# Two layer-norm entries and the row products of a feed-forward, put in another order in a two-layer hybrid network

## The chip, the cores and the metric

The kernel runs on one core of a Trainium2 chip. The metric is device time in microseconds (us) of one execution; the kernel before takes 2463.92 us, the median of three runs.

TensorE (PE) multiplies, VectorE (DVE), ScalarE (ACT) and GpSimd (POOL) do the rest, and SyncE (SP) issues most transfers. Each engine works through its own queue in order.

## The reference

The network has two layers on 256 latent and 256 context tokens of width 1024. The first mixes with multi-head latent attention, the second with a gated delta rule; each ends in a gated feed-forward of width 2816. A second part of the second layer ("block 2") follows. What matters here is how a layer wraps its mixer: both residual additions are post-normalised and gated by rows that come from a conditioning vector, and the result is modulated before the next matmul.

```
y = layer_norm(alpha * x + gate * mixer(h), ln_g, ln_b)     # alpha = (2 * DEPTH) ** 0.25
h = modulate(y, shift, scale)                               # y * (1 + scale) + shift
z = layer_norm(alpha * y + gate2 * swiglu(h), ln2_g, ln2_b)

def layer_norm(x, g, b):
    mu = mean(x); var = mean((x - mu) ** 2)
    return (x - mu) * rsqrt(var + 1e-5) * g + b
```

The six rows of each layer (shift, scale and gate, twice) are products of the conditioning vector with a matrix of 1024 x 1024 for each row.

## The kernel before

Tokens are worked in tiles of 128 rows. Every weight and every activation that goes into a matmul is split into a high and a low part: `split` (L119) casts the high part on ScalarE (L125) and subtracts it on VectorE (L126). A product is then three matmuls: high by high (L159), low by high (L160), high by low (L161).

**A layer-norm entry.** `resid` (L520 and on) multiplies the projection by the gate (`y`, L524), adds it to the residual (L526, or L528), and takes the statistics of 512 columns (L530), twice for a tile. `ln_norm` (L334) aggregates them (`BN_AGGR`, L329), scales the variance (L165, VectorE), takes its power of -1/2 on GpSimd (L166; `self.pow` is that instruction), makes the bias -mean * r on VectorE (L338), and normalises the tile in place on ScalarE (L339). `mod_in` (L310) transposes the tile on PE in two groups of four (L317), modulates each block on its way out of PSUM, in turn on VectorE (L324) and ScalarE (L322), into a scratch tile `half`, and splits it (`xh`, `xl`). The plain layer-norm rows are applied to the residual later, by `ln_affine` (L341): four slices, a multiply and an addition each on GpSimd (L345, L346), in place, after the transposes have read the tile.

**Where it happens.** In layer 0 there are four token tiles `res_2401` to `res_2404`, in pairs; `ln` inside `layer0` does a pair. `fin1`, `late` and `fin2` call it: the entry to layer 0's feed-forward (stages `fin1`, `late`), and the entry of the delta-rule layer (`fin2`). In layer 1 two streams, one for each tile (`t` of 0 and 1: `x_11602`, `x_11603`), run `st_all`; its `post1` is the entry of the feed-forward, and `mid` the affine step after it.

**Row products.** The conditioning rows of the next layer are made beside layer 0's feed-forward. `mod_tick` (L271) loads a matrix of 128 x 1024 (`mraw`, SyncE's queue, three buffers) and multiplies it by the broadcast conditioning row on VectorE with an accumulator (`mjunk`, L281). These products get a lower priority (`later(200)`) and are put in the queue behind the instruction in `self.hold`. The feed-forward works in units of hidden columns: weight splits (`lo`), hidden product `hf` (L183) and its split (`hl`). At the start of each unit `step` asks for 5 or 8 products.

**What sets the order.** A scheduler orders each engine's instructions by priority and by its own estimate of when the operands are there; `high_priority` raises a block, and `issue_after(i)` sets a block behind instruction i in that order. The scheduler works on the whole program, so an edge at one place can move instructions of other places.

Of the kernel before, what the change touches and what calls it, by code (L numbers as in the profile page):

```python
# [30 lines left out]
class Net:  # L31
# [88 lines left out]
    def split(self, src, hi, lo, hi_eng=None):  # L120
        nc = self.nc
        if hi_eng == "v":
            nc.vector.tensor_copy(hi, src)
        else:
            nc.scalar.copy(hi, src)  # L125
        self.tail = nc.vector.tensor_tensor(lo, src, hi.bitcast(F32), ALU.subtract).ins  # L126

    def wload(self, src, A, B, parts=2, local=False, raw=None):
# [205 lines left out]
    def ln_norm(self, x, st):  # L334
        nc = self.nc
        m, r = self.ln_stats(st)
        nb = self.tiny(1, "p_nbias")
        nc.vector.scalar_tensor_tensor(nb, m, -1.0, r, ALU.mult, ALU.mult)  # L338
        nc.scalar.activation(x, x, AF.Identity, bias=nb, scale=r)  # L339

    def ln_affine(self, x, g, b):  # L341
# [268 lines left out]
    def layer0(self, stk):  # L610
        nc, a = self.nc, self.a
        sid = [1, 1, 0, 0]
        xT = self.first_in()
        self.crow = [self.mp.tile([P, D], F32, name=f"crow{i}") for i in range(2)]
        for r, src in zip(self.crow, (a["c"][0], a["c_ctx"])):
            nc.scalar.dma_start(r, src.unsqueeze(0).to_broadcast([P, D]))
            nc.scalar.activation(r, r, AF.Silu)
        j2 = self.mod_start(0, 2)
        j3 = self.mod_start(0, 3)
        j45 = []  # L620

        def mid():
            j45.extend(self.mod_start(0, c) for c in (4, 5))

        def step(i):
            self.hold = self.tail
            self.mod_tick(1)

        oT = self.mla(xT, mid, step)
        m2, m3, m4, m5 = j2, j3, *j45  # L630
        pool = stk.enter_context(self.tc.tile_pool(name="res1", bufs=1, reuse_waits="tile"))
        res = [pool.tile([P, D], F32, name=f"res{s}") for s in range(4)]
        for s in range(4):
            nc.sync.dma_start(res[s], a["x" if s > 1 else "ctx"][(s % 2) * P:(s % 2) * P + P])
        with self.phase("l0b"):
            def ln(pair, acc, lnrow, ab, first):
                for i in range(2):
                    s = 2 * pair + i
                    st = self.bn_st()
                    self.resid(res[s], acc[i], gates[s], first, st)  # L640
                    self.ln_norm(res[s], st)
                    self.mod_in(res[s], oT, s * P, ab, sid[s])
                if lnrow:
                    with self.tc.issue_after(self.pow):
                        for s in (2 * pair, 2 * pair + 1):
                            self.ln_affine(res[s], *lnrow)

            ln1 = self.row(a["ln1_g"][0]), self.row(a["ln1_b"][0])
            while self.mq and self.mq[0][1] < 5:
                self.mod_tick(1)  # L650
            ab = self.mod_ab(m3, m4, (0, 0))
            gr = [self.gate_row(m2, s) for s in range(2)]
            gates = [gr[i] for i in sid]
            held = []

            def fin1(pair, acc):
                if pair == 0:
                    ln(pair, acc, ln1, ab, True)
                else:
                    held.append(acc)  # L660

            def late():
                ln(1, held[0], ln1, ab, True)
                self.hold = self.tail
                jn.extend(self.mod_start(1, c) for c in range(2))
                gr = [self.gate_row(m5, s) for s in range(2)]
                gates[:] = [gr[i] for i in sid]

                ln2.extend([self.row(a["ln2_g"][0]), self.row(a["ln2_b"][0])])

            def fin2(pair, acc):
                ln(pair, acc, ln2 if pair else None, ab2, False)

            def step(u):
                if u == NU // 2:
                    jl.extend(self.mod_start(1, c, (0,)) for c in range(2, 6))
                self.mod_tick(5 if u < NU // 2 else 8)
                if u == NU // 2:
                    ab2.extend(self.mod_ab(*jn, (0, 1)))

            jn, jl, ln2, ab2 = [], [], [], []
            self.out_pairs(oT, a["mla_out"], KD, fin1)
            self.ffn512(oT, a["w_ffg"], a["w_ffu"], a["w_ffd0"], res, gates, late, step, fin2)
            self.mods1 = jl
        self.hl = self.dp.tile([NT * P, D], F32, name="hl_spill")
        for t in range(NT):
            nc.gpsimd.dma_start(self.hl[t * P:(t + 1) * P], res[2 + t])
        return oT
# [495 lines left out]
    def st_all(self, t):  # L1184
# [7 lines left out]
        def post1(acc):  # L1192
            with self.tc.high_priority():
                st = self.bn_st()
                self.resid(x, acc, gate(m2), True, st)
                self.ln_norm(x, st)
                self.mod_in(x, self.xT, t * P, ab(), 0)

        def mid():
            self.ln_affine(x, *rows("ln1"))  # L1200
# [668 lines left out]
```

## Time and profile before

| | |
|---|---|
| runs, us | 2463.92, 2468.24, 2463.59 |
| profiled execution, us | 2464.18 |
| its span, us | 2462.4 |
| mean granted TensorE clock | 0.977 |
| busy share: PE, DVE, ACT, POOL | 94%, 70%, 51%, 9% |
| row products (L281) | 128, 156.0 us in all |

The attention layer runs to about 250 us, layer 0's projection and feed-forward to about 673, the delta-rule layer to about 1196, and the rest is layer 1's feed-forward and block 2. The span is the time from the first to the last instruction; the device time has a little around it. A long busy share of PE says how little there is to gain on the whole, and the idle time in a timeline says where it stands.

### The profile page before, as it was taken

How to read it: one execution, taken by the hardware profiler on the slowest of the kernel's cores; microseconds unless marked ns; L12 is line 12 of the kernel's file. 1: busy time of each engine (PE TensorE's matmuls, PEld its weight loads, DVE VectorE, ACT ScalarE, POOL GpSimd, SP SyncE). 2: the span in 40 equal slices, each digit the busy share in tenths (PEclk: the TensorE clock that was granted, in tenths of full speed). 3: DMA queues.
4: the chain of work that ended last, by engine and by line, in shares of the span. 5: the costliest groups of instructions: out<-in, count | busy, mean ns of one | idle time of the engine just before them, and what ended most of it. 6: DMA issues, size and time to landing. Idle time of an engine off the chain costs nothing. (4 is left out here: it accounts for less than half of the span.)

```text
span 2462.4 us, 38477 instructions
## 1 busy us (share of the span) xinstructions
PE 2325.2 (94%) x14542; PEld 1929.3 (78%) x14542; DVE 1729.3 (70%) x3312; ACT 1263.1 (51%) x2668; POOL 212.2 (9%) x297
## 2 busy tenths in 40 slices
PE   7999999999898999979899999999999999999998
PEld 4978888778777878878688788877788788777786
DVE  6886899875769879785655665577655565687554
ACT  6376422222375675855554455564655554655553
POOL 0000500000231020211300000001000000001000
PEclk9999999999999999999999999998999999999999
DMA  8554256652123121222665565541655455414552
GB/s 298 190 159 171 86 190 207 218 184 69 50 75 91 57 70 44 78 95 70 219 203 174 168 200 177 167 129 61 200 185 190 161 189 187 146 45 131 195 196 95
DMA packets 94515, 358.22 MB, mean 145 GB/s; under 512 B 12633, under 2 KB 13817, under 8 KB 87545
## 3 DMA queue, kind: packets, MB, share of 16 engines
q1 hardware_dynamic: 88544, 343.91, 42.1%
q0 software_dynamic: 2336, 5.84, 0.9%
q10 hardware_dynamic: 3448, 6.02, 0.7%
q8 instruction: 114, 1.87, 0.3%
q14 instruction: 73, 0.59, 0.1%
HBM read 348.77 MB, written 3.67 MB: 143 GB/s over the span
## 5 line engine op out<-in xcount | busy, mean ns | idle before, releaser
L125 ACT CAST hi<-raw 128x512 fp32r<-128x512 f32 (+3 forms) x740 | 488.0, 701 | 443.3 <-DMA raw<-in_w_gu 121.1
L126 DVE TENSOR_TENSOR lo<-raw,hi 128x512 fp32r<-128x512 f32 (+3 forms) x740 | 558.6, 789 | 210.6 <-ACT hi L125 206.2
L159 PE MATMUL g<-hi,xh 128*128 128x512 f32 (+1 forms) x1120 | 416.5, 372 | 17.6 <-DVE hid L1295 6.2
L161 PE MATMUL g<-hi,xl 128*128 128x512 f32 (+1 forms) x1120 | 405.8, 363 | 2.4 <-DVE xl L1260 2.1
L160 PE MATMUL g<-lo,xh 128*128 128x512 f32 (+1 forms) x1120 | 406.0, 363 | 1.1 <-DVE lo L126 1.1
L159 PE MATMUL g<-xh,hi 128*128 128x512 f32 (+1 forms) x776 | 276.2, 356 | 1.7 <-ACT cvu L775 1.7
L161 PE MATMUL g<-xh,lo 128*128 128x512 f32 (+1 forms) x776 | 275.8, 355 | 1.4 <-DVE lo L126 1.4
L160 PE MATMUL g<-xl,hi 128*128 128x512 f32 (+1 forms) x776 | 275.0, 354 | 0.0
L159 PEld LDWEIGHTS g<-hi,xh 128*128 128x128 f32 x1120 | 213.5, 191 | 53.1 <-DVE hid L1295 8.4
L161 PEld LDWEIGHTS g<-hi,xl 128*128 128x128 f32 x1120 | 212.9, 190 | 37.1 <-DVE xl L1260 4.8
L160 PEld LDWEIGHTS g<-lo,xh 128*128 128x128 f32 x1120 | 213.7, 191 | 31.3 <-DVE lo L126 2.6
L159 PE MATMUL acc<-xh,hh 128*128 128x512 f32 x440 | 174.5, 397 | 8.3 <-ACT hh L125 6.6
L126 DVE TENSOR_TENSOR xl<-raw,xh 128x512 fp32r<-128x512 f32 (+1 forms) x223 | 153.9, 701 | 27.8 <-ACT xh L125 27.5
L160 PE MATMUL acc<-xl,hh 128*128 128x512 f32 x440 | 171.9, 391 | 0.0
L161 PE MATMUL acc<-xh,hl 128*128 128x512 f32 x440 | 171.7, 395 | 0.2 <-DVE hl L126 0.2
L159 PEld LDWEIGHTS g<-xh,hi 128*128 128x128 f32 x776 | 148.5, 191 | 21.0 <-ACT cvu L775 2.1
L161 PEld LDWEIGHTS g<-xh,lo 128*128 128x128 f32 x776 | 148.1, 191 | 20.2 <-DVE lo L126 1.6
L161 PE MATMUL acc<-hi,xl 128*128 128x512 f32 (+2 forms) x432 | 160.2, 374 | 3.3 <-DVE xl L1260 3.3
L160 PEld LDWEIGHTS g<-xl,hi 128*128 128x128 f32 x776 | 148.1, 191 | 18.9 <-issue 0.4
L159 PE MATMUL acc<-hi,xh 128*128 128x512 f32 (+2 forms) x432 | 161.6, 377 | 0.2 <-ACT hi L125 0.2
L160 PE MATMUL acc<-lo,xh 128*128 128x512 f32 (+2 forms) x432 | 160.8, 373 | 0.0
L281 DVE SCALAR_TENSOR_TENSOR mjunk<-mraw,crow 128x1024 f32<-128x1024 f32 x128 | 156.0, 1219 | 1.3
(576 smaller groups left out, 4022.4 us busy)
## 6 DMA issues: line engine op xcount, KB each, us to landing
raw<-in_w_gu SPq DMA_DIRECT2D x220, 512.0 KB, 4.5
raw<-in_w_down SPq DMA_DIRECT2D x88, 512.0 KB, 4.4
mraw<-in_w_modb SPq DMA_DIRECT2D x80, 512.0 KB, 4.5
raw<-in_w_in SPq DMA_DIRECT2D x28, 512.0 KB, 4.3
raw<-in_w_ffg SPq DMA_DIRECT2D x11, 1024.0 KB, 4.9
raw<-in_w_ffu SPq DMA_DIRECT2D x11, 1024.0 KB, 5.1
raw<-in_w_ffd SPq DMA_DIRECT2D x11, 1024.0 KB, 4.9
raw<-in_w_ffd SPq DMA_DIRECT2D x22, 512.0 KB, 4.4
```

Of the source, the lines that this page charges most:

```text
L125: nc.scalar.copy(hi, src)
L126: self.tail = nc.vector.tensor_tensor(lo, src, hi.bitcast(F32), ALU.subtract).ins
L159: nc.tensor.matmul(out, lh, rh, start=start, stop=False)
L160: nc.tensor.matmul(out, lh, rl, start=False, stop=False)
L161: nc.tensor.matmul(out, ll, rh, start=False, stop=stop)
L281: nc.vector.scalar_tensor_tensor(junk, raw, 1.0, self.crow[s], ALU.mult, ALU.mult, accum_out=m[:, j, s:s + 1])
```

## The change

`split` and `ln_norm` keep the high cast (`self.lead`) and the bias instruction (`self.nb`) for later use. In layer 0 both tiles' residuals and norms are written before either tile's `mod_in`. In `step`, from the second unit on, the row products are set behind the last low split written so far. In layer 1's `post1` the second tile's residual is set behind the first tile's bias, and its norm behind the first tile's last high cast. The amount of work is the same.

```diff
@@ split
-            nc.scalar.copy(hi, src)
+            self.lead = nc.scalar.copy(hi, src).ins
@@ ln_norm
-        nc.vector.scalar_tensor_tensor(nb, m, -1.0, r, ALU.mult, ALU.mult)
+        self.nb = nc.vector.scalar_tensor_tensor(nb, m, -1.0, r, ALU.mult, ALU.mult).ins
@@ layer0, ln
-                for i in range(2):
-                    s = 2 * pair + i
-                    st = self.bn_st()
-                    self.resid(res[s], acc[i], gates[s], first, st)
-                    self.ln_norm(res[s], st)
+                ss = (2 * pair, 2 * pair + 1)
+                sts = [self.bn_st() for _ in ss]
+                for i, s in enumerate(ss):
+                    self.resid(res[s], acc[i], gates[s], first, sts[i])
+                    self.ln_norm(res[s], sts[i])
+                for s in ss:
                     self.mod_in(res[s], oT, s * P, ab, sid[s])
@@ layer0, step
+                if u:
+                    self.hold = self.tail
@@ st_all, post1
-                self.resid(x, acc, gate(m2), True, st)
-                self.ln_norm(x, st)
+                with self.tc.issue_after(self.nb) if t else nullcontext():
+                    self.resid(x, acc, gate(m2), True, st)
+                with self.tc.issue_after(self.lead1) if t else nullcontext():
+                    self.ln_norm(x, st)
                 self.mod_in(x, self.xT, t * P, ab(), 0)
+                self.lead1 = self.lead
```

Lines behind the change stand 3 to 6 further down in the new kernel; names keep their numbers except for some scratch tiles.

**First place: VectorE in the first unit of layer 0's feed-forward, second half.** `lo` is a weight's low split, `mjunk` a row product, `hf` and `hl` the hidden product and its split. Before:

```order
L126 TENSOR_TENSOR lo_3298<-raw_3295,hi_3297 128x1024
L281 SCALAR_TENSOR_TENSOR mjunk_3259,modcol_3021<-mraw_3255,crow_394 128x1024
L281 SCALAR_TENSOR_TENSOR mjunk_3263,modcol_3021<-mraw_3261,crow_393 128x1024
L183 TENSOR_TENSOR hf_3152<-hf_3152,g_3103 128x256
L126 TENSOR_TENSOR lo_3302<-raw_3295,hi_3301 128x1024
L126 TENSOR_TENSOR hl_3156<-hf_3152,hh_3155 128x256
L281 SCALAR_TENSOR_TENSOR mjunk_3265,modcol_3021<-mraw_3261,crow_394 128x1024
L281 SCALAR_TENSOR_TENSOR mjunk_3269,modcol_3021<-mraw_3267,crow_393 128x1024
L281 SCALAR_TENSOR_TENSOR mjunk_3271,modcol_3021<-mraw_3267,crow_394 128x1024
L183 TENSOR_TENSOR hf_3208<-hf_3208,g_3159 128x256
L281 SCALAR_TENSOR_TENSOR mjunk_3275,modcol_3021<-mraw_3273,crow_393 128x1024
L126 TENSOR_TENSOR hl_3212<-hf_3208,hh_3211 128x256
```

And now, from the same weight split on:

```order
L126 TENSOR_TENSOR lo_3298<-raw_3295,hi_3297 128x1024
L126 TENSOR_TENSOR lo_3302<-raw_3295,hi_3301 128x1024
L183 TENSOR_TENSOR hf_3152<-hf_3152,g_3103 128x256
L126 TENSOR_TENSOR hl_3156<-hf_3152,hh_3155 128x256
L183 TENSOR_TENSOR hf_3208<-hf_3208,g_3159 128x256
L126 TENSOR_TENSOR hl_3212<-hf_3208,hh_3211 128x256
L281 SCALAR_TENSOR_TENSOR mjunk_3257,modcol_3021<-mraw_3255,crow_393 128x1024
```

Six products have left the stretch up to the second hidden split, and one more that stood just in front of it; the first of them stands right behind that split now, the others in the next unit, and the last products of all stand in the eighth unit after the first, where the seventh was the last before.

**Second place: VectorE at the entry of layer 1, first tile.** `x_11603`, `y_11902`, `y_11906` and `t_11901` are the second tile's; `t_11733` is the first tile's scaled variance, `t_11736` its bias. Before:

```order
L524 TENSOR_TENSOR y_11902<-acc_11295,row_11622 128x512
L329 BN_AGGR t_11730<-t_11721 128x2
L126 TENSOR_TENSOR lo_11790<-raw_11787,hi_11789 128x512
L526 SCALAR_TENSOR_TENSOR x_11603<-x_11603,y_11902 128x512
L524 TENSOR_TENSOR y_11906<-acc_11296,row_11622 128x512
L530 BN_STATS t_11901<-x_11603 128x6
L526 SCALAR_TENSOR_TENSOR x_11603<-x_11603,y_11906 128x512
L165 TENSOR_SCALAR t_11733<-t_11730 128x1
L126 TENSOR_TENSOR lo_11790<-raw_11787,hi_11789 128x512
L530 BN_STATS t_11901<-x_11603 128x6
L338 SCALAR_TENSOR_TENSOR t_11736<-t_11730,t_11732 128x1
```

And now:

```order
L329 BN_AGGR t_11730<-t_11721 128x2
L126 TENSOR_TENSOR lo_11790<-raw_11787,hi_11789 128x512
L165 TENSOR_SCALAR t_11733<-t_11730 128x1
L126 TENSOR_TENSOR lo_11790<-raw_11787,hi_11789 128x512
L338 SCALAR_TENSOR_TENSOR t_11736<-t_11730,t_11732 128x1
L524 TENSOR_TENSOR y_11902<-acc_11295,row_11622 128x512
L524 TENSOR_TENSOR y_11906<-acc_11296,row_11622 128x512
L526 SCALAR_TENSOR_TENSOR x_11603<-x_11603,y_11902 128x512
L526 SCALAR_TENSOR_TENSOR x_11603<-x_11603,y_11906 128x512
L530 BN_STATS t_11901<-x_11603 128x6 x2
```

The second tile's operations have moved from in front of the first tile's bias to behind it.

**Third place: GpSimd and VectorE at the same entry, second tile.** `t_11732` and `t_11912` are the two powers, `row_12487` and `row_12489` the layer-norm rows. GpSimd before:

```order
L166 TENSOR_TENSOR t_11732<-t_11733,mhalf 128x1
L166 TENSOR_TENSOR t_11912<-t_11913,mhalf 128x1
L345 TENSOR_TENSOR x_11602<-x_11602,row_12487 128x256
L346 TENSOR_TENSOR x_11602<-x_11602,row_12489 128x256
L345 TENSOR_TENSOR x_11602<-x_11602,row_12487 128x256
L346 TENSOR_TENSOR x_11602<-x_11602,row_12489 128x256
L345 TENSOR_TENSOR x_11602<-x_11602,row_12487 128x256 x2
L346 TENSOR_TENSOR x_11602<-x_11602,row_12489 128x256 x2
```

GpSimd now:

```order
L166 TENSOR_TENSOR t_11732<-t_11733,mhalf 128x1
L345 TENSOR_TENSOR x_11602<-x_11602,row_12487 128x256 x2
L346 TENSOR_TENSOR x_11602<-x_11602,row_12489 128x256 x2
L345 TENSOR_TENSOR x_11602<-x_11602,row_12487 128x256 x2
L346 TENSOR_TENSOR x_11602<-x_11602,row_12489 128x256 x2
L166 TENSOR_TENSOR t_11912<-t_11913,mhalf 128x1
```

The eight affine slices of the first tile have moved in front of the second tile's power. VectorE, where `t_11916` is the second tile's bias, `halfA_11744` and `halfA_11756` the first tile's modulated blocks; now:

```order
L329 BN_AGGR t_11910<-t_11901 128x2
L324 TENSOR_SCALAR halfA_11756<-t_11751,modA_11635,modB_11636 128x128
L165 TENSOR_SCALAR t_11913<-t_11910 128x1
L126 TENSOR_TENSOR lo_11826<-raw_11823,hi_11825 128x512
L338 SCALAR_TENSOR_TENSOR t_11916<-t_11910,t_11912 128x1
L324 TENSOR_SCALAR halfA_11744<-t_11739,modA_11635,modB_11636 128x128
L324 TENSOR_SCALAR halfA_11756<-t_11751,modA_11635,modB_11636 128x128
L126 TENSOR_TENSOR lo_11826<-raw_11823,hi_11825 128x512
L126 TENSOR_TENSOR lo_11834<-raw_11831,hi_11833 128x512
L126 TENSOR_TENSOR xl_6187<-halfA_11744,xh_6186 128x4x128
L126 TENSOR_TENSOR xl_6187<-halfA_11756,xh_6186 128x4x128
```

Before, that bias stood in front of all four `halfA` rows and between the two splits `lo_11834`; now the last two `halfA` rows, three weight splits and the low splits of the first tile stand behind it.

## Rows read from the trace of the kernel before

**Rows 1.** The summary page, part 1: busy us (share of the span) xinstructions.

```profile
PE 2325.2 (94%) x14542; PEld 1929.3 (78%) x14542; DVE 1729.3 (70%) x3312; ACT 1263.1 (51%) x2668; POOL 212.2 (9%) x297
```

**Rows 2.** Windows: length, busy time (x count) of each engine, clock, DMA.

```profile
300.00:350.00 50.00, 47.94 (x256) 41.08 (x255) 49.34 (x74) 13.97 (x18) 4.12 (x4) 1.00 0.61 211
700.00:750.00 50.00, 44.07 (x276) 37.77 (x275) 36.43 (x69) 33.30 (x87) 14.61 (x20) 0.94 0.21 63
```

**Rows 3.** Timeline of PE, layer 0's feed-forward: start, duration, instruction, [idle before <-releaser].

```profile
316.87 0.50 PE L159 MATMUL acc<-hi,hh 128*128 128x512 f32 x1 [2.06 <-ACT hh L125]
...
512.07 0.50 PE L159 MATMUL acc<-hi,hh 128*128 128x512 f32 x1 [1.51 <-ACT hh L125]
```

**Rows 4.** Timeline of PE, entry of the delta-rule layer.

```profile
669.56 1.97 PE L317 MATMUL t<-ident,res 128*128 128x128 f32 x8 [5.19 <-ACT res L339]
...
673.59 0.69 PE L159 MATMUL acc<-xh,hi 128*64 128x512 f32 x1 [2.05 <-ACT xh L125]
```

**Rows 5.** Timeline of PE, entry of layer 1.

```profile
1201.76 1.97 PE L317 MATMUL t<-ident,x 128*128 128x128 f32 x8 [5.50 <-ACT x L339]
...
1207.33 0.79 PE L159 MATMUL g<-hi,xh 128*128 128x512 f32 x1 [3.60 <-ACT xh L125]
```

**Rows 6.** Timeline of DVE, layer 0's feed-forward.

```profile
312.28 1.22 DVE L281 SCALAR_TENSOR_TENSOR mjunk<-mraw,crow 128x1024 f32<-128x1024 f32 x1
...
508.39 1.22 DVE L126 TENSOR_TENSOR lo<-raw,hi 128x1024 fp32r<-128x1024 f32 x1 [4.13 <-ACT hi L125]
```

**Rows 7.** Timeline of ACT, entry of the delta-rule layer.

```profile
667.24 1.12 ACT L125 CAST xh<-half 128x512 fp32r<-128x512 f32 x2
...
668.27 1.24 ACT L339 ACTIVATE res<-res,t,t 128x1024 f32<-128x1024 f32 x1
```

**Rows 8.** Timeline of DVE, entry of the delta-rule layer.

```profile
667.88 2.33 DVE L126 TENSOR_TENSOR xl<-half,xh 128x512 fp32r<-128x512 f32 x2
...
670.72 0.41 DVE L324 TENSOR_SCALAR half<-t,modA,modB 128x128 f32<-128x128 f32 x1 [0.50 <-PE t L317]
```

**Rows 9.** Timeline of PE, gates of the delta rule and after.

```profile
692.08 0.39 PE L159 MATMUL g<-xh,hi 128*128 128x256 f32 x1 [0.42 <-ACT cvu L775]
...
694.71 0.46 PE L715 MATMUL acc<-ident,half 64*128 64x64 f32 x4 [1.54 <-DVE half L712]
...
743.22 0.58 PE L159 MATMUL g<-hi,xh 128*128 128x256 f32 x1 [4.05 <-ACT cvu L775]
```

**Rows 10.** Timeline of ACT, gates of the delta rule.

```profile
697.73 1.28 ACT L727 ACT_TABLE_LOAD   x1
699.02 0.28 ACT L727 ACTIVATE eg<-acc 128x128 f32<-128x128 f32 x1
```

**Rows 11.** Timeline of DVE, entry of layer 1.

```profile
1195.35 0.68 DVE L524 TENSOR_TENSOR y<-acc,row 128x512 f32<-128x512 f32 x1
...
1199.02 0.15 DVE L165 TENSOR_SCALAR t<-t 128x1 f32<-128x1 f32 x1
...
1200.29 0.14 DVE L338 SCALAR_TENSOR_TENSOR t<-t,t 128x1 f32<-128x1 f32 x1
...
1202.82 0.68 DVE L338 SCALAR_TENSOR_TENSOR t<-t,t 128x1 f32<-128x1 f32 x1 [0.45 <-POOL t L166]
...
1204.02 0.72 DVE L324 TENSOR_SCALAR halfA<-t,modA,modB 128x128 f32<-128x128 f32 x2
```

**Rows 12.** Timeline of ACT, entry of layer 1.

```profile
1197.66 1.14 ACT L125 CAST hi<-raw 128x512 fp32r<-128x512 f32 x2 [0.91 <-DMA raw<-in_w_gu]
...
1204.68 0.79 ACT L322 ACTIVATE halfA<-t,modB,modA 128x128 f32<-128x128 f32 x2
```

**Rows 13.** Timeline of POOL, entry of layer 1.

```profile
1199.25 0.95 POOL L166 TENSOR_TENSOR t<-t,mhalf 128x1 f32<-128x1 f32 x1 [3.22 <-DVE t L165]
...
1202.76 0.72 POOL L345 TENSOR_TENSOR x<-x,row 128x256 f32<-128x256 f32 x1
...
1208.03 2.32 POOL L346 TENSOR_TENSOR x<-x,row 128x256 f32<-128x256 f32 x2
```

## The prediction, made before the change was run

> **What bounds the kernel now.** I read the summary page first: PE is busy for 2325.2 us, 94% of the span [rows 1], so all its idle time together is about 137 us, and anything the change can give or take has to pass through that. The next view is the timeline of PE with the idle time ahead of each matmul, to find where in the changed places PE stands, and what released it. There are three. In layer 0's feed-forward VectorE is the crowded engine: 49.34 us busy of 50 [rows 2], and PE waits there a few times for the high half of the hidden units, the longest 2.06 and 1.51 us [rows 3]. At the entry of the delta-rule layer PE waits 5.19 us for the normalised rows and then 2.05 us for a cast [rows 4]. At the entry of layer 1's feed-forward it waits 5.50 and 3.60 us in the same way [rows 5]. The last view is the timeline of VectorE, ScalarE and GpSimd around those stops, where the reader sees what stood ahead of the operation waited for. The bound is thus PE everywhere else, and a chain of VectorE, GpSimd and ScalarE at the entries.
>
> The sum is made against the profiled execution, 2464.18 us (span 2462.4 us and 1.8 us around it), which lies 0.26 us above the median of 2463.92. A change of under 0.2%, 4.9 us, is about what a measurement of this kernel cannot tell from none.
>
> **Products behind the previous unit's split.** No product goes or comes: the same number of VectorE rows stands in both orders. What moves is where they stand. In the first unit 7 of them stood ahead of the second hidden split, each 1.22 us long [rows 6]; now none does, so 8.5 us leave that stretch. The wait of 2.06 us for the hidden cast [rows 3] stood behind three of them in a row, and I take it as gone: -2.06. The 8.5 us do not vanish: the products run about one unit later, and reach one unit further than they did. In the second unit 4 now stand ahead of a hidden product where 2 stood, up to 2 x 1.22 = 2.4 us more there; PE had no wait at that place, so a part is covered by matmuls. The last unit that now holds products gets a wait like the one in the seventh, 1.51 us at most [rows 3]. I put +1.1 for both, between nothing and 2.4. SyncE's queue changes too: weight loads now stand ahead of the product rows' loads. VectorE stood 4.13 us before a weight's split [rows 6], behind a cast and that load; if this is what made the 1.51 us, it may go as well. Sum of this part: -1.0, between -3.6 (both waits go, nothing comes) and +2.4.
>
> **Layer norms of layer 0.** In three of the four pairs the order on VectorE, ScalarE and GpSimd is as before: nothing. In the last pair the second tile's normalising activation, which started at 668.27 behind both casts of the first tile [rows 7], now stands ahead of the first tile's last halves and casts. It can start some 1.9 us sooner, so the transposes (669.56) come sooner. But the first tile's casts (1.12 us for two) then end about 1.0 us later, and the two low splits behind them, 2.33 us [rows 8], with them, at about 671.2; on VectorE they stand ahead of the second tile's halves, which began at 670.72. PE's next matmul, at 673.59 [rows 4], waits for a cast of these halves: +0.4. If the low splits run faster with GpSimd idle it may be -1.5, and +1.5 if the casts slip by the whole activation (1.24 us).
>
> **The delta-rule layer's first part.** The change has no line there, but the scheduler's order moves. The chain of the gates is pulled forward: 9 matmuls fewer stand ahead of its transposes on PE. Seven such matmuls took from 692.08 to 693.17, 0.156 each (694.71 less its wait of 1.54) [rows 9], so 1.4 us of cover go, while the operand comes about 0.45 us sooner, since one row of a product of the depthwise filter and a cast moved behind the chain: +0.95. ScalarE loads its table 3 times more in the whole program (37 for 34), 1.28 us each [rows 10], 3.84 in all, beside matmuls where PE does not wait for it. On the other side the gates end sooner, and a wait such as the 4.05 us at 743.22 [rows 9] may shrink. I take +1.0, nearest to the one piece that I can place, between -5.9 (all of PE's idle time from 700 to 750, 50 less 44.07 [rows 2]) and +4.8 (0.95 and all three loads).
> After a table load the next activation starts at 699.02, right when the load that began at 697.73 is done [rows 10]. The Trainium skill ("ScalarE: Activation LUTs", What ACT_TABLE_LOAD costs) gives about 1.28 us for the load and 1.38 us for a drain beside it; the first agrees with the row, the second does not show there. By that page three loads would be 8.0 us, and the upper end 8.9 instead of 4.8, an estimate from its figure; the row decides.
>
> **Entry of layer 1.** First tile: ahead of the scaling of its variance (1199.02) stood five operations of the second tile, which follow each other by 0.60 us (a y began at 1195.35), and they now stand behind its bias [rows 11]; the scaling comes 5 x 0.60 = 3.0 us sooner, at about 1196.05. From there to the bias took 1.27 us (1199.02 to 1200.29), through GpSimd's power: bias at 1197.3. The activation cannot use all of it: the first of two weight casts, which starts at 1197.66 when its load lands, 0.57 us [rows 12], stands ahead of it: 1198.23. The activation takes 1.24 us, as at 668.27 [rows 7], and the transposes follow at about 1199.53 instead of 1201.76 [rows 5]: 2.23 us sooner.
>
> Second tile: here a wait is added. GpSimd did both tiles' powers (the first at 1199.25, the second done when the bias at 1202.82 [rows 11] could start) and then the eight affine operations on the first tile [rows 13]. Now the eight stand between the two powers. They wait for the transposes, so the first starts at about 1200.1. One took 0.72 us alone (1202.76) and 1.16 beside a busy VectorE (1208.03, two in 2.32) [rows 13]. VectorE is busy until about 1202.6 with the second tile's six operations from 1197.4 on (3.6 us), two halves, the aggregate, the scaling and a weight split, and then waits, so three at 1.16 and five at 0.72 make 7.1 us: 1207.2. The power behind them, 0.95 as in the row at 1199.25, ends at about 1208.1. The second tile's bias on VectorE waits for it, and queued behind this bias are the last halves of the first tile, two weight splits and the first tile's low splits. ScalarE's last halves and casts wait for those halves. From the power's end: 0.14 for the bias and 0.36 for a half (0.72 for two at 1204.02) on VectorE [rows 11], then two halves (0.79) and a cast (half of 1.14) on ScalarE [rows 12], and some 0.1 from engine to engine: 2.0 us, so PE's first weight matmul starts at about 1210.1 instead of 1207.33 [rows 5]: +2.8. Below: eight at 0.72 give 5.8 us, and +1.5. Above: eight at 1.16 give 9.3, and +5.0. That the matmuls behind such a wait are slower (0.79 for the first [rows 5]) I count as before. The next weights' loads wait for a split that is late by 6 us too; the hidden activation behind their casts is then about in time, +1 at worst.
>
> **Sum.** -1.0 + 0.4 + 1.0 + 2.8 = +3.2; 2464.18 + 3.2 = 2467.4, and 0.26 less for the median: 2467.
>
> **Rivals.** The first ends on the faster side: the delta-rule layer gains. Its gates feed everything behind them, and within their chain 20 matmuls and transposes stood on PE ahead of the last group where 3 stand now, so they end up to 17 x 0.156 = 2.7 us sooner. If what follows is limited by them, the waits of the next stretch go: from 700 to 750 PE is busy for 44.07 of 50 us [rows 2], so at most 5.9 us. It decides from the point where that term falls below -3.2. In full: -1.0 + 0.4 - 5.9 + 2.8 = -3.7, 2460. For it: the wait of 4.05 us stands in that stretch [rows 9]. Against: it is a wait for a copy out of a projection, not for the gates. Chance 0.27.
> The second is slower beyond the bound, by GpSimd alone: the eight affine operations run at 1.16 throughout, and the weight casts behind them hold the hidden activation by the +1: -1.0 + 0.4 + 1.0 + 6.0 = +6.4, 2470. For it: the two in 2.32 us ran so [rows 13]. Against: VectorE stands while it waits for them. Chance 0.20.
> The third: the change's new queue on GpSimd costs nothing, because PE's first weight matmul waits for something else by then, and only the sooner transposes count: -2.2 at this entry, the sum -1.8, 2462. For it: that wait after the transposes was 3.60 us before too, with several operations in it. Against: the halves behind the second bias are part of the operand. Chance 0.13.
> My forecast, a slight loss from one new wait on GpSimd: 0.40.
>
> **How the numbers follow.** The forecast and the third rival lie within 0.2% (2459.0 to 2468.8 about the median); of the forecast's 0.40 about 0.13 lies above, of the first rival's 0.27 about 0.16 below, of the second's 0.20 about 0.15 above, and of the third's 0.02 below: faster 0.18, same 0.54, slower 0.28. The range leaves out about a tenth at each end: 2458 to 2472.5, the forecast's own 2464 to 2470.
>
> **What would show it.** In the profile after: PE's transposes at layer 1's entry about 2 us sooner behind the end of the projection, and its first weight matmul 2 to 3 us later; on GpSimd eight affine operations in front of the second power, and VectorE idle for about 5 us before the second bias, released by GpSimd. In layer 0's first unit no wait of 2 us for the hidden cast, and products in the eighth unit. I am wrong on layer 1 if the gap before the first weight matmul is not longer, and on the rest if the delta-rule layer's stretch differs by more than 4 us.

## The result and the profile after

The changed kernel takes 2475.09 us, the median of 13 runs (2466.06 to 2482.02), against 2463.03 for the kernel before in 13 runs beside it: a ratio of 1.0054 [1.0040, 1.0068], 0.54% slower. The prediction was 2467 with a range to 2472.5, a loss of 0.13%; the loss is four times that and lies outside the range.

The profiled execution took 2481.59 us (span 2479.8), 6.5 us above its own median, and that of before 1.15 us above its median. The spans thus differ by 17.4 us and the medians by 12.1: the rows below place the loss, and overstate its size by some 5 us, of which 3.9 arise ahead of any changed instruction (the first L317 transposes start at 257.6 us before and 261.5 after; the kernels of the experiments below start them anywhere between 256 and 262).

The first line of the page after, beside [rows 1]: the same 14542 matmuls take 4.0 us more, and ACT has 3 instructions more, the table loads.

```profile
PE 2329.2 (94%) x14542; PEld 1929.6 (78%) x14542; DVE 1730.7 (70%) x3312; ACT 1267.4 (51%) x2671; POOL 212.5 (9%) x297
```

By stages: the start +3.9; layer 0 from the first to the last L317 transpose 413.5 us before, 409.3 after (-4.3); from there to the delta-rule layer's first weight matmul +1.4; the delta-rule layer with its projection +16.2 (below); layer 1's entry +1.0; what comes behind -0.8. One profile of each kernel shows layer 0's -4.3; with the products alone (an experiment below) that stretch is 0.8 us shorter.

**Layer 0.** Windows of the changed kernel, as in [rows 2] (length, busy time and count of each engine, clock, DMA share, GB/s). In the first unit PE is busy for all 50 us where it was for 47.94, since VectorE has lost its products there; in the stretch of the gates it is busy for 4 us less.

```profile
300.00:350.00 50.00, 50.00 (x267) 42.98 (x266) 44.82 (x65) 17.11 (x25) 8.00 (x9) 1.00 0.51 179
700.00:750.00 50.00, 40.08 (x226) 33.01 (x222) 37.42 (x67) 36.96 (x90) 15.76 (x20) 0.91 0.25 75
```

VectorE in that unit, beside [rows 6]: the first product stands behind the second hidden split (hl), and each split starts 0.47 us after VectorE was free, released by the hidden cast.

```profile
313.41 0.43 DVE L126 TENSOR_TENSOR hl<-hf,hh 128x256 fp32r<-128x256 f32 x1 [0.47 <-ACT hh L125]
...
317.49 0.43 DVE L126 TENSOR_TENSOR hl<-hf,hh 128x256 fp32r<-128x256 f32 x1 [0.47 <-ACT hh L125]
317.84 1.22 DVE L281 SCALAR_TENSOR_TENSOR mjunk<-mraw,crow 128x1024 f32<-128x1024 f32 x1
```

PE's waits from 250 to 640 us (total, times, longest), before and then after. The 2.06 us of [rows 3] are gone; the 1.51 us are now 1.24.

```profile
PE acc L159 <- ACT hh L125: 5.7, 5, 2.1
```

```profile
PE acc L159 <- ACT hh L125: 3.1, 3, 1.2
```

**Entry of the delta-rule layer.** PE after, beside [rows 4]: the transposes wait 4.05 us where they waited 5.19 (now for a scratch half, no longer for the normalised rows), the first weight matmul 3.42 where it waited 2.05.

```profile
669.22 1.94 PE L317 MATMUL t<-ident,res 128*128 128x128 f32 x8 [4.05 <-ACT half L322]
674.58 0.69 PE L159 MATMUL acc<-xh,hi 128*64 128x512 f32 x1 [3.42 <-ACT xh L125]
```

**The delta-rule layer.** Its length is read from four marks: the first weight matmul above, and the last group of `acc<-S,kT` in each of three recurrences (before 872.25, 969.97 and 1080.65; after 880.05, 980.82 and 1097.76), up to the last of the second tile's transposes behind layer 1's entry. The four stretches took 198.7, 97.7, 110.7 and 139.0 us before, and 205.5, 100.8, 116.9 and 140.1 after: 546.1 and 563.3, so +17.2. The last stretch holds layer 1's entry and its +1.0; up to the end of the layer's projection it is +16.2. That is nearly the whole difference of the spans, in a layer in which the change has no line but its entry. PE's first such mark, before and then after:

```profile
872.25 1.06 PE L1002 MATMUL acc<-S,kT 128*128 128x128 f32 x8
```

```profile
880.05 1.06 PE L1005 MATMUL acc<-S,kT 128*128 128x128 f32 x8
```

ScalarE in the first stretch, before and then after. `xv<-acc,gbias` is an exponential of the decays (32 in a group), `cvy<-cvy` (L780, after L783) a SiLU, `cvu<-g` the copy of a value projection into its filter.

```profile
716.06 1.28 ACT L957 ACT_TABLE_LOAD   x1
...
734.36 0.82 ACT L777 ACTIVATE cvy<-cvu,gcw 128x512 f32<-128x512 f32 x1
...
742.58 0.59 ACT L775 COPY cvu<-g 128x512 f32<-128x512 f32 x1 [2.92 <-DVE cvy L779]
```

```profile
716.38 1.28 ACT L960 ACT_TABLE_LOAD   x1
...
719.39 1.28 ACT L783 ACT_TABLE_LOAD   x1
720.69 0.42 ACT L783 ACTIVATE cvy<-cvy 128x256 f32<-128x256 f32 x1
...
726.12 1.28 ACT L960 ACT_TABLE_LOAD   x1
727.42 0.89 ACT L960 ACTIVATE xv<-acc,gbias 128x128 f32<-128x128 f32 x3
...
739.40 1.40 ACT L780 ACTIVATE cvy<-cvu,gcw 128x512 f32<-128x512 f32 x2
...
747.84 0.59 ACT L778 COPY cvu<-g 128x512 f32<-128x512 f32 x1 [6.09 <-DVE cvy L782]
```

Here the reader sees the first place of the loss. Three exponentials are done, then one SiLU of a query filter stands in the queue, with a load in front and one behind. The other 29 exponentials begin at 727.42, and the value filters behind them, whose first tap (the product with one coefficient) is ScalarE's, at 739.40 instead of 734.36. The other taps are VectorE's, and the next `cvu` copy waits for them; VectorE, which also multiplies with the exponentials, is busy for 14.7 of the 15 us from 735 on. Its first tap, before and then after:

```profile
738.10 0.75 DVE L779 SCALAR_TENSOR_TENSOR cvy<-cvu,gcw,cvy 128x512 f32<-128x512 f32 x1
```

```profile
742.91 0.74 DVE L782 SCALAR_TENSOR_TENSOR cvy<-cvu,gcw,cvy 128x512 f32<-128x512 f32 x1
```

The copy then stands at 747.84 instead of 742.58, and PE waits for it, 7.58 us where [rows 9] had 4.05:

```profile
748.48 0.58 PE L159 MATMUL g<-hi,xh 128*128 128x256 f32 x1 [7.58 <-ACT cvu L778]
```

The second place stands some 50 us later. The scheduler orders the whole program with the loads in its estimate; it now puts the next group's key transposes (`t<-ident,ktok`) behind the merge of the triangular inverses (32 x 32 matmuls): at 813.39 us, where they stood at 786.55. Their rows, before and then after:

```profile
786.55 0.66 PE L912 MATMUL t<-ident,ktok 128*128 128x128 f32 x4 [1.10 <-DVE ktok L908]
```

```profile
813.39 0.66 PE L915 MATMUL t<-ident,ktok 128*128 128x128 f32 x4
```

Windows over the two places, before and then after:

```profile
735.00:750.00 15.00, 10.95 (x64) 9.91 (x63) 14.62 (x33) 6.18 (x9) 0.77 (x2) 0.89 0.12 36
...
795.00:810.00 15.00, 13.28 (x410) 11.75 (x409) 11.27 (x16) 11.86 (x21) 6.40 (x9) 0.82 0.52 130
```

```profile
735.00:750.00 15.00, 7.42 (x34) 6.06 (x33) 14.72 (x32) 8.88 (x19) 3.22 (x4) 0.80 0.23 71
...
795.00:810.00 15.00, 11.41 (x192) 9.29 (x186) 2.63 (x6) 4.38 (x9) 1.63 (x1) 0.54 0.32 83
```

From 795 to 810 PE is granted 0.54, nearly all the time the lower of its two levels (1.2 GHz, 0.50 in the rows), and VectorE has almost nothing to do (2.63 us). PE's rows of the merge, before and then after (the last in each is its last round of 64 x 64 matmuls):

```profile
796.95 2.12 PE L1128 MATMUL acc<-big,Mt 32*32 32x32 f32 x128 [0.38 <-DVE big L1108]
...
811.99 3.37 PE L1128 MATMUL acc<-Mt,xv 64*64 64x64 f32 x64
```

```profile
789.52 2.12 PE L1131 MATMUL acc<-big,Mt 32*32 32x32 f32 x128 [1.31 <-DVE big L1111]
...
800.12 0.21 PE L1131 MATMUL acc<-big,xv 32*32 32x32 f32 x1 [3.59 <-issue]
...
811.38 2.08 PE L1131 MATMUL acc<-Mt,xv 64*64 64x64 f32 x64
```

The first round (128 matmuls) takes 2.12 us in both. Then the clock falls: after, it is 1.00 until 790 and 0.50 from 792 to 809, behind a wait of 1.31 us and that round; before, it fell at about 805, when the second round was done, and was low until 815. So nearly all of the first 64 matmuls of 64 x 64 ran at the lower level in both kernels, and the last 64 only in the kernel before: 3.37 us, and 2.08 at the full clock. ScalarE copies a result out behind the first round, and another behind the first half of the 64 x 64 matmuls (`xv<-acc`), before and then after:

```profile
799.45 0.59 ACT L1136 COPY xv<-acc 128x512 f32<-128x512 f32 x1
...
807.21 0.59 ACT L1161 COPY xv<-acc 128x512 f32<-128x512 f32 x1 [1.70 <-PE acc L1128]
```

```profile
791.74 0.59 ACT L1139 COPY xv<-acc 128x512 f32<-128x512 f32 x1
...
806.08 0.59 ACT L1164 COPY xv<-acc 128x512 f32<-128x512 f32 x1 [2.73 <-PE acc L1131]
```

From the one to the other it is 7.8 us before and 14.3 after: +6.6, about what the whole first stretch lost (+6.8). PE is idle for 2.3 us more of it, and busy for 4.3 more: the lower clock, and eight matmuls of 512 columns that now stand between the rounds. The merge itself had begun 7.7 us sooner than before, since the keys' work now stood behind it, and that work is still to do at 806; so the 6.6 is not the price of the merge. Of the +16.2 us in PE's time from the start of the layer to the end of its projection (522.7 and 538.9 us), 7.7 are idle time (46.3 and 54.0) and 8.5 busy time of the same 4552 matmuls, at a mean granted clock of 0.94 where it was 0.96.

The two places lie in the first stretch. The other 9.3 us stand in the second (+3.1) and the third (+6.2). In the third PE is idle for 2.5 us more, and most of that is one wait of transposes for a SiLU; as PE's waits in that stretch list it (total, times, longest), before and then after:

```profile
PE t L899 <- ACT cvy L780: 0.6, 1, 0.6
```

```profile
PE t L902 <- ACT cvy L783: 2.3, 1, 2.3
```

The rest of these two stretches is not traced to a row.

**Layer 1's entry.** PE, beside [rows 5]:

```profile
1216.18 1.09 PE L317 MATMUL t<-ident,x 128*128 128x128 f32 x8 [2.70 <-ACT x L339]
...
1225.56 0.79 PE L159 MATMUL g<-hi,xh 128*128 128x512 f32 x1 [8.28 <-ACT xh L125]
```

GpSimd, beside [rows 13], and the second bias on VectorE, beside [rows 11]:

```profile
1213.66 1.01 POOL L166 TENSOR_TENSOR t<-t,mhalf 128x1 f32<-128x1 f32 x1
1216.76 1.77 POOL L345 TENSOR_TENSOR x<-x,row 128x256 f32<-128x256 f32 x2 [2.09 <-ACT hi L125]
...
1221.72 1.40 POOL L346 TENSOR_TENSOR x<-x,row 128x256 f32<-128x256 f32 x2
1223.08 0.56 POOL L166 TENSOR_TENSOR t<-t,mhalf 128x1 f32<-128x1 f32 x1
```

```profile
1223.67 0.16 DVE L338 SCALAR_TENSOR_TENSOR t<-t,t 128x1 f32<-128x1 f32 x1 [3.86 <-POOL t L166]
```

The transposes come 2.70 us behind the projection's matmuls instead of 5.50, the eight affine operations stand in front of the second power, and VectorE stands 3.86 us for it. From the end of the projection to the first weight matmul: 11.07 us before, 12.08 after.

### The profile page after: what moved, and what is told of

It is laid out like the page before. It is cut to its first block, busy times and chain, and to the rows that moved or that the text cites. A ratio compares the mean times of both kernels' runs of the same rounds, so it can differ in the third digit from the quotient of the medians.

```text
span 2479.8 us, 38502 instructions
## 1 busy us (share of the span) xinstructions
PE 2329.2 (94%) x14542; PEld 1929.6 (78%) x14542; DVE 1730.7 (70%) x3312; ACT 1267.4 (51%) x2671; POOL 212.5 (9%) x297
```

## The experiments

The letters are those of the expectations. In the first four runs, **A**: the layer norms of layer 0 make the loss, by the order that they bring about in the delta-rule layer, and the other two edits do what their own stages show; what stands against it in a run, **B** or **C**, its expectation says. Then, within A, **T**: ScalarE's table loads; **K**: the late key transposes; **G**: the chain of the gates, pulled forward. A ratio is against the kernel before on the same chip, with its 95% interval; each kernel has 5 to 12 runs. The measure "merge" is the time between the two copies named above, in the one profiled execution.

**The layer norms alone.** Of the change only the new `ln` in `layer0` is kept.

```diff
...
-                    self.resid(res[s], acc[i], gates[s], first, st)
-                    self.ln_norm(res[s], st)
...
+                for i, s in enumerate(ss):
+                    self.resid(res[s], acc[i], gates[s], first, sts[i])
+                    self.ln_norm(res[s], sts[i])
+                for s in ss:
                     self.mod_in(res[s], oT, s * P, ab, sid[s])
```

> The kernel before with the rewritten ln of layer 0 alone; its order differs from before only in the delta-rule layer, where it is that of the changed kernel. Theory A (the loss is that new order in the delta-rule layer, 539 us from its first matmul to its last in the trace of after against 523): 0.5 to 0.8% slower than before, 2475 to 2482 us, slower than the whole change by the few us that the two other edits give. Rival B (the loss comes from the entry of layer 1, or from the row products): no change, within 0.2%.

Measured: 1.0058 [1.0036, 1.0081]. The whole loss is there. Its rows in the delta-rule layer are those of the whole change: stretches of 205.1, 101.1, 115.3 and 140.3 us, merge 14.4, PE idle for 53.3 us up to the end of the projection.

**The products alone.**

```diff
+                if u:
+                    self.hold = self.tail
```

> The kernel before with the row products behind a unit's split alone; its order differs from before in layer 0's feed-forward and nowhere else. Theory A: 2 to 4 us faster than before (the stage from the first layer-norm transposes to the last took 409.2 us after and 413.5 before), so 0.1 to 0.2% faster. Rival B (the products that come later cost as much as the wait that goes): no change, below 1 us.

Measured: 1.0002 [0.9988, 1.0016]. No difference that can be told, as its B had it.

**Layer 1's entry alone.** The two `issue_after` in `post1` and the two names that they need.

```diff
+                with self.tc.issue_after(self.nb) if t else nullcontext():
+                    self.resid(x, acc, gate(m2), True, st)
+                with self.tc.issue_after(self.lead1) if t else nullcontext():
+                    self.ln_norm(x, st)
```

> The kernel before with the edges in the layer 1 entry alone; the order differs from before only there. Theory A: about 1 us slower (from the last projection matmul to the first weight matmul 12.1 us after, 11.1 before), not to be told from no change. Rival B (what waits behind GpSimd's affine operations costs more than that gap shows, in the loads behind it): 3 us slower or more.

Measured: 1.0007 [0.9992, 1.0023]. The interval holds A's 1 us and B's 3 us both, but not 0.5%: as the cause of the loss GpSimd's queue falls.

**Both without the layer norms.** The last two diffs together; `ln` is as before.

> Both edits without the rewritten ln: the delta-rule layer has the order of before. Theory A: 1 to 4 us faster than before, some 12 to 16 us faster than the whole change. Rival C (the loss of the change is not in the delta-rule layer's order but in where code and buffers lie, or in the start): slower than before like the whole change, by 0.3% or more.

Measured: 0.9997 [0.9979, 1.0014]. The gain of 1 to 4 us cannot be told, and C falls. In the order of the instructions, too, the layer norms alone move what stands in the delta-rule layer (more than a thousand of PE's 12315 rows); the products alone move only layer 0's feed-forward, layer 1's entry only itself. The pair that does it is the last call of `ln`.

**The SiLU in front of the exponentials** (layer norms as in the first run).

```diff
-        nc.scalar.activation(y, y, AF.Silu)
+        self.qs = nc.scalar.activation(y, y, AF.Silu).ins
...
+        self.qk = self.qs        # behind the query loop
...
+                    with self.tc.issue_after(self.qk) if b == 0 else nullcontext():
                         nc.scalar.activation(Db[:, c, :], ..., AF.Exp, ...)
```

> The rewritten ln alone, plus one edge: the first head group's decay exponentials are put behind the SiLU of its second query filter (in the kernel before the same edge changes no row of any order). The order then has no table load among these exponentials (2 with ln alone), the next group's key transposes stand early again as in the kernel before, and the gates' chain stays pulled forward. Theory T (the two table loads in the middle of the exponentials, and what queues behind them) and theory K (the next group's keys come 27 us late, so less of its work is there to fill PE) both: 10 to 16 us less than ln alone, within 0.2% of before. Theory G (the gates' chain pulled forward with little cover): as slow as ln alone, 0.5% over before.

Measured: 1.0015 [1.0000, 1.0031]. Most of the loss is gone although the gates' chain is still forward, so G falls as its main cause. The rows of ScalarE show one load ahead of the exponentials and the next behind them; the `cvu` copy that stood behind the filters comes at 734.19:

```profile
716.01 1.28 ACT L960 ACT_TABLE_LOAD   x1
...
734.19 0.61 ACT L776 COPY cvu<-g 128x512 f32<-128x512 f32 x1
...
735.86 1.28 ACT L781 ACT_TABLE_LOAD   x1
```

PE's longest wait for a `cvu` copy there is 1.4 us. Its profile is the fastest of its 12 runs (2453.45), with a first stretch of 191.3 us and a merge of 7.0.

**Loads kept, keys early** (the layer norms, and the value part's priority).

```diff
-        with self.later(300):
+        with self.later(350):
             v = self.gdn_v(0, xT)
```

The scheduler then leaves two loads among the exponentials, but puts the key transposes near their old place.

> The rewritten ln alone, with the first group's value projections at a slightly lower priority (350 for 300): the two table loads among the exponentials stay, the gates' chain stays forward, but the next group's key transposes stand early (row 3862 of PE's order; 4037 with ln alone, 3806 before). Theory K: 8 us or more less than ln alone, near the time before. Theory T and theory G: as slow as ln alone, 0.4 to 0.6% over before.

Measured: 1.0039 [1.0026, 1.0053]. That lies at the lower end of what T expected, and not near the time before, as K expected; the interval overlaps that of the layer norms alone. The wait for `cvu` is there, while the first stretch is 197.9 us and the merge 10.5:

```profile
744.13 0.58 PE L159 MATMUL g<-hi,xh 128*128 128x256 f32 x1 [7.10 <-ACT cvu L776]
```

**Keys later still, in the kernel before** (the same line, `later(600)`).

> The kernel before without any edit of the change, the first group's value projections at priority 600 instead of 300: two table loads among the exponentials, the next group's key transposes late (row 4058), the gates' chain where it was. Theories T and K: 0.3 to 0.7% slower than before. Theory G: within 0.2%.

Measured: 1.0126 [1.0110, 1.0143], a first stretch of 221.5 us. The expectation was missed: the loss is about twice what T and K allowed. It has two loads as well, so it tells nothing of K by itself.

**Another order, no loads, keys early, in the kernel before** (the same line, `later(350)`, without the layer norms): the control.

> A control: the kernel before with priority 350 instead of 300. Some 1300 of PE's 12315 rows stand elsewhere in the delta-rule layer, but there is no table load among the exponentials and the next group's keys stand early (row 3801). Theories T, K and G: within 0.2% of before. If any reordering of this layer costs, 0.3% slower or more.

Measured: 1.0036 [1.0023, 1.0049]. The expectation was missed. An order without either mark costs 0.36%: in its profile the second stretch is 103.4 us instead of 97.7, the merge 11.1. Neither T nor K has this.

**The loads added to the kernel before.** A SiLU of one column behind the third exponential, and the other 29 behind it; none of the change's lines.

```diff
...
+                        with self.tc.issue_after(e.ins):
+                            self.dum = nc.scalar.activation(self.gtmp[:, 0, 0, 0:1], self.ones[:, 0:1], AF.Silu).ins
...
```

> The kernel before with one added SiLU of 128 x 1 behind the third exponential of the first head group: two table loads more (36 for 34), and the scheduler, which counts them, then puts the next group's key transposes late (row 4045) as in the changed kernel; the entry of the delta-rule layer and the gates stand as before. Theory T (one misplaced SiLU among the exponentials, with the order that the scheduler makes around it, is the main cost of the change): 0.3 to 0.7% slower than before. If only the new entry or the gates cost: within 0.2%.

Measured: 1.0060 [1.0038, 1.0082]. This is the whole loss, from one misplaced operation and the order that the scheduler then makes (its key transposes are late too). Its rows repeat those of the changed kernel: ScalarE, then PE, then the second window.

```profile
721.42 1.28 ACT L961 ACT_TABLE_LOAD   x1
...
725.90 1.28 ACT L958 ACT_TABLE_LOAD   x1
...
747.09 0.59 ACT L775 COPY cvu<-g 128x512 f32<-128x512 f32 x1 [5.69 <-DVE cvy L779]
```

```profile
747.73 0.58 PE L159 MATMUL g<-hi,xh 128*128 128x256 f32 x1 [7.65 <-ACT cvu L775]
```

```profile
795.00:810.00 15.00, 11.34 (x164) 9.20 (x158) 5.32 (x7) 6.31 (x10) 0.68 (x1) 0.58 0.18 52
```

**The loads taken away from the layer norms.** The second query filter of the first group gets a copy in place of its SiLU, which leaves that SiLU out of the computation.

```diff
-        nc.scalar.activation(y, y, AF.Silu)
+        nc.scalar.activation(y, y, AF.Copy if self.qskip else AF.Silu)
...
```

> The rewritten ln alone, with the first group's second query filter passed on by a copy instead of its SiLU (this leaves that SiLU out of the computation), so that no table load stands among the exponentials; the same edit in the kernel before changes no row of its order. The gates stay pulled forward, the next group's keys stand early again (row 3805), the value filters stay behind the 32 exponentials. Theory T: 8 us or more less than ln alone, what is left over before being the third group's 4 to 5 us (that stretch is 69 us with every rewritten ln so far, 64.3 with the order of before). Theory G (the gates): as slow as ln alone.

Measured: 1.0021 [1.0001, 1.0041]. Two thirds of the loss go with this one operation and the order around it. The wait for `cvu` is 3.90 us again, the merge 6.9, and the clock does not fall around it:

```profile
795.00:810.00 15.00, 14.19 (x367) 12.41 (x366) 7.81 (x14) 11.33 (x20) 3.16 (x5) 1.00 0.26 61
```

**The whole change with the SiLU in front** (the edge of the fifth run).

> The whole change with the edge that puts the exponentials behind the SiLU. Theory T: about 10 us less than the whole change, 0 to 0.2% over before, since the edits of layer 0's row products and of layer 1's entry move the time by less than can be told. If the three edits gain together what they did not alone: faster than before by 0.2% or more.

Measured: 1.0002 [0.9985, 1.0019]. The loss is gone, and there is no gain: without its side effect the change is worth nothing that can be told (0.2% either way could not). Its merge is 10.7 us and PE's busy time in the layer is 4.7 us above that of before, at the same total time: from one profile these figures carry that much chance.

**Late keys without loads, in the kernel before** (`later(1200)` on the key product of the second group).

```diff
+            with self.later(1200) if b == 1 else nullcontext():
                 nc.vector.tensor_tensor(kt[:, j], pt[j]..., ALU.mult)
```

> The kernel before with the product that makes the second head group's normalised keys at a priority 1200 lower: its key transposes stand late (row 4011), like in the changed kernel (4037), but no table load stands among the exponentials (34 in all) and the gates and the entry are as before. It parts what came together so far. Theory K (the late keys cost, the loads only bring them about): 0.3% or more slower than before, the stretch from the first matmul of the delta-rule layer to the end of the first recurrence 5 us or more over the 198.7 of before. Theory T in its narrow form (the loads themselves cost, through the exponentials and the value filters behind them): within 0.2%, that stretch within 3 us of before.

Measured: 1.0030 [1.0015, 1.0045]. K wanted at least 5 us more in the first stretch and T at most 3; the profile shows 200.1 us, +1.4, as T has it, but that profile is the lowest of its runs. The ratio is K's 0.3%, with an interval that reaches down into T's 0.2%. So neither is borne out in full. In the windows the clock falls here as well, but PE has work throughout:

```profile
795.00:810.00 15.00, 14.86 (x397) 12.59 (x398) 7.01 (x11) 6.82 (x12) 4.50 (x7) 0.57 0.33 71
```

Set side by side (all but the ratio from one profile each; the loads are those among the 32 exponentials, the keys' time is that of their first transposes, PE's idle time runs from the layer's first weight matmul to the end of its projection):

| | loads | keys at, us | ratio | first stretch, us | merge, us | PE idle, us |
|---|---|---|---|---|---|---|
| before | 0 | 786.6 | 1 | 198.7 | 7.8 | 46.3 |
| layer norms alone | 2 | 812.5 | 1.0058 | 205.1 | 14.4 | 53.3 |
| loads added to before | 2 | 812.6 | 1.0060 | 207.3 | 14.6 | 53.9 |
| keys later still, in before | 2 | 824.8 | 1.0126 | 221.5 | 11.8 | 58.3 |
| loads kept, keys early | 2 | 787.2 | 1.0039 | 197.9 | 10.5 | 52.8 |
| late keys without loads | 0 | 802.6 | 1.0030 | 200.1 | 10.5 | 47.6 |
| loads taken away | 0 | 784.6 | 1.0021 | 192.8 | 6.9 | 50.3 |
| SiLU in front | 0 | 781.4 | 1.0015 | 191.3 | 7.0 | 50.9 |
| another order (control) | 0 | 790.0 | 1.0036 | 196.2 | 11.1 | 48.1 |
| whole change, SiLU in front | 0 | 783.4 | 1.0002 | 199.8 | 10.7 | 47.3 |

Shown: the loss comes from the layer norms' order alone, one SiLU among the exponentials with the order made around it brings it back into the kernel before, and taking it away or moving it removes most or all of it. Not settled: how it divides between the loads and the late keys. Each alone comes out at 0.3 to 0.4%, which would add up, but the control has neither and costs as much. PE's idle time in the layer goes with the loads (52.8 us and more with two, 50.9 and less without, 47.6 with late keys alone), but idle time is not the whole loss. Each of these edits moves many rows besides its own, so no run takes one mark alone. Open too: the third stretch is 115 us or more instead of 111 in all kernels with the new layer norms and in the one with the added loads, and also where the loads are gone (a wait for a SiLU of 2.3 to 2.8 us stands there in each of them); and PE's 3.6 us within the merge, which the profile lays to nothing it records and which stand in the changed kernel, with the layer norms alone and with the added loads.

## Why the prediction was wrong

**Products, -1.0.** The mechanism held: the products left the first unit, the wait of 2.06 us went, and PE's waits for the hidden cast fell by 2.6 us, from 5.7 to 3.1. The other end was over-feared, as no new wait of that kind came in the later units. In time it cannot be told (1.0002 [0.9988, 1.0016]).

**Layer norms of layer 0, +0.4.** The transposes came sooner and the first matmul behind them later, as worked out: their two waits sum to 7.47 us (4.05 and 3.42) and were 7.24 [rows 4], so +0.2 at that place. The loss did not arise there, but this edit's order brought it (1.0058 alone).

**The delta-rule layer's first part, +1.0 (-5.9 to +4.8).** This is the step that failed. The whole layer measured +16.2 us in the profile, and the layer norms' order alone, whose effect lies in this layer, cost 1.0058, as much as the whole change. I followed the new order for the gates' nine matmuls, and then priced the rest by a count: three table loads at 1.28 us, "beside matmuls where PE does not wait for it". The runs showed the place and the order around it to matter, and not the sum (two loads added to the kernel before, 2.6 us, cost 0.60%): two of them with one SiLU between stood in front of 29 exponentials and the value filters, and PE's wait for the copy behind these grew from 4.05 us [rows 9] to 7.58. That wait was the row that should have warned me: it hung on the queue into which the loads went, by way of VectorE's part of the filter. And the upper end was made of the changed instructions alone. The order moved more than a thousand rows of PE; the late keys, the longer second and third stretches, and the lower granted clock had no term at all. How the loss divides among these stays open.

**Entry of layer 1, +2.8 (+1.5 to +5.0).** The mechanism was right in each part, and the size too large: +1.0. The activation did not stand behind the weight cast, so the transposes came 2.70 us behind the projection and not 3.27; eight affine operations took 6.3 us (1216.76 to 1223.08) and not 7.1; the power behind them 0.56 us, while VectorE stood, and not the 0.95 of [rows 13]. The prediction's "0.72 us alone" was misread: VectorE worked at that time, on the bias that took 0.68 us at 1202.82 [rows 11]; that the operations beside a standing VectorE then took 0.70 was luck. In time it cannot be told (1.0007 [0.9992, 1.0023]).

**The rivals.** The first, a gain of 5.9 us in the delta-rule layer, had the right place and the wrong sign. The second had the right sign and the wrong place: layer 1's entry. The third, no new cost at layer 1's entry, is not borne out: the +1.0 is there, if too small to be told in time. I had said I would be wrong "if the delta-rule layer's stretch differs by more than 4 us"; it did. "Slower" had 0.28.

## What to carry to other kernels

When a scheduler moves a thousand rows, the edit's own lines can be the smallest part of its price, as here: look first in the new order for an operation that has come to stand among others of another table or kind, and ask which wait of the profile hangs on that queue; a wait of 4 us already there warns that little hides a delay. Such a misplacement can be undone with one ordering edge, and should be before the edit itself is judged: here that took back the whole 0.5%, and showed that the edit was worth nothing that could be told. And try a control order, since here an order with none of the suspected marks cost 0.36%.

## What the runs showed of the hardware

In the changed kernel PE waited 1.31 us, ran 128 matmuls of 32 x 32 in 2.12 us, and then the granted clock stood at its lower level from 792 to 809 us. What the lower level costs shows in the merge's last round, 64 matmuls of 64 x 64: 3.37 us in the kernel before, where the clock was low until 815, and 2.08 in the changed one, where it had risen again. In this pair of profiles 8.5 of the layer's 16.2 us are the same matmuls in more busy time, at a mean granted clock of 0.94 instead of 0.96.

An activation follows its table load at once (719.39 and 1.28 us of load, then 720.69), as in [rows 10], so two loads around one SiLU took 2.6 us of ScalarE. The kernel before with two such loads added, and the order made around them, is 0.60% slower, some 15 us.

GpSimd's affine operations took 0.9 to 0.95 us each while VectorE worked and 0.70 when it stood (two in 1.77 and in 1.91, then two in 1.40), and its power 1.01 and then 0.56 us.
